# RMSNorm with every row doubled, on one core: two stores split so that the next load can reuse the buffer early

## Chip, cores, metric

One core of a Trainium2 chip. The metric is the device time of one execution in microseconds (us). One program is run several times; "span" is the profiled part of one execution, about 2 us shorter than the time.

## Reference

```python
x: [8, 512, 2048] float32, gamma: [2048] float32
x_rep  = np.repeat(x, 2, axis=1)                       # every row twice
rms    = np.sqrt((x_rep ** 2).mean(axis=-1, keepdims=True) + 1e-6)
output = x_rep / rms * gamma                            # [8, 1024, 2048]
```

So 33.55 MB are read and 67.11 MB written, with little arithmetic between.

## The kernel before

The 4096 rows are cut into eight tiles of 128 partitions times 4 rows. A tile's buffer holds eight rows (64 KB) per partition: x is loaded into rows 4 to 7, the scaled rows are written to rows 0, 2, 4, 6 and copied to 1, 3, 5, 7, and one transfer of 8.39 MB stores all eight. There are three buffers. All transfers are issued from SyncE, in one queue.

```python
K = 4; R = 2
rows = ctx.enter_context(tc.tile_pool(name="rows", bufs=3))

def new_tile():
    ys.append(rows.tile([P, K * R, D], f32, name="y"))

def load(i, k0, k1):
    nc.sync.dma_start(
        out=ys[i][:, K * (R - 1) + k0 : K * (R - 1) + k1, :], in_=x_t[i, :, k0:k1, :]
    )

def store(i):
    nc.sync.dma_start(out=out_t[i], in_=ys[i].rearrange("p j d -> p (j d)"))
# ... total, square, reduce, root, scale, repeat: the arithmetic ...

cuts = [0, *range(D // 4, D + 1, D // 8)]          # seven pieces of gamma
load(0, 0, H)
for c0, c1 in zip(cuts[:-2], cuts[1:-1]):
    gamma_piece(c0, c1)
load(0, H, K)
gamma_piece(cuts[-2], cuts[-1])
# ... gamma is spread over the partitions by TensorE ...
load(1, 0, K)
load(2, 0, K)
# ...
by_rows(0, whole)                                   # each of these ends in store(i)
two = mixed(sums(1, 1), shared, ahead=(2, 1))
mixed(two, shared)
for j in (3, 4, 5):
    new_tile()                                      # the buffers of 0, 1, 2
    load(j, 0, K)
by_rows(3, shared)
_, _, ss = mixed(sums(4, H), whole, ahead=(5, 0))
for j in (6, 7):
    new_tile()                                      # the buffers of 3, 4
    load(j, 0, K)
# ... tile 5 in another way, then tiles 6 and 7 ...
```

## Time and profile before

| | before |
|---|---|
| time, median of the first 3 runs | 239.29 us (239.11 to 239.78) |
| span | 237.1 us |
| busiest engine | VectorE, 132.9 us |
| queue's packets, share of 16 engines' span | 98.6% |

Bytes over the span is 425 GB/s, and the row of transfer engines is full. Whether the transfers leave holes is read from the order of issues and landings, which the prediction shows. Besides the page the trace holds a record of each packet (start, duration, size) and of each increment of a semaphore (a counter on which engines wait) by a transfer; 16 increments, one from each transfer engine, make one landing.

In the lines of profiles below, SP is SyncE, ACT ScalarE and DVE VectorE, and a q behind a name stands for what that engine issues. A line of a timeline gives start and duration in us, engine, line of the kernel, operation, output<-input and count; brackets hold the idle time before, and what ended it. A line of waits gives the total in us, the number of waits and the longest.

### The profile page before, as it was taken

The page shows a single profiled execution, that of the slowest core. Times are in us where ns is not written, and L with a number is a line of the kernel's source. Part 1 is how long each engine was busy: PE and PEld are TensorE (multiplying, and loading weights), DVE is VectorE, ACT ScalarE, POOL GpSimd, SP SyncE. Part 2 cuts the span into 40 slices and gives each one's busy share as a digit, 9 for nine tenths or more (in the row PEclk, how much of TensorE's full clock was granted, in tenths as well). Part 3 has the DMA queues.
Part 4 walks back from the last instruction along what each step waited for, and adds up shares of the span by engine and source line. Part 5 has one row for each costly group of instructions (what it writes and reads, how often), then busy time and mean ns, then how long its engine had stood idle before and what let it go on. Part 6 is the DMA issues. An engine that isn't in the chain of part 4 may idle for free. (4 is left out here: it accounts for less than half of the span.)

```text
span 237.1 us, 246 instructions
## 1 busy us (share of the span) xinstructions
PE 7.2 (3%) x8; PEld 2.3 (1%) x8; DVE 132.9 (56%) x45; ACT 92.6 (39%) x48; POOL 13.0 (5%) x20
## 2 busy tenths in 40 slices
PE   0650000000000000000000000000000000000000
PEld 0210000000000000000000000000000000000000
DVE  0049997997950000039979994094067997980000
ACT  2681957600600000098995003900599760230000
POOL 0000002002000000000020002005302002000000
DMA  7999999899898989999998989899998989899994
GB/s 263 441 448 442 437 448 509 376 398 486 354 531 354 531 354 431 398 415 437 442 531 354 531 354 509 376 387 415 437 531 354 531 354 509 376 486 398 420 464 177
DMA packets 2462, 100.67 MB, mean 425 GB/s; under 512 B 279, under 2 KB 285, under 8 KB 286
## 3 DMA queue, kind: packets, MB, share of 16 engines
q1 hardware_dynamic: 2462, 100.67, 98.6%
HBM read 33.56 MB, written 67.11 MB: 425 GB/s over the span
## 5 line engine op out<-in xcount | busy, mean ns | idle before, releaser
L87 DVE SCALAR_TENSOR_TENSOR y<-y,ss,gamma_b 128x2048 f32<-128x2048 f32 x28 | 64.7, 2345 | 10.4 <-POOL ss L83 7.4
L74 DVE TENSOR_REDUCE ss<-y 128x3 f32<-128x6144 f32 (+2 forms) x6 | 41.4, 6902 | 10.9 <-ACT y L69 10.9
L69 ACT ACTIVATE y<-y 128x6144 f32<-128x6144 f32 (+2 forms) x6 | 33.6, 5604 | 22.9 <-DMA y<-in_x_dram 22.9
L63 ACT ACTIVATE sq<-y 128x2048 f32<-128x2048 f32 x13 | 24.4, 1875 | 42.1 <-DMA y<-in_x_dram 41.9
L94 ACT COPY y<-y 128x4096 f32<-128x4096 f32 (+1 forms) x7 | 23.5, 3358 | 32.1 <-DVE y L87 32.1
L140 DVE RECIPROCAL ss<-ss 128x2 f32<-128x2 f32 x4 | 0.6, 161 | 49.0 <-ACT ss L139 49.0
L94 DVE COPY y<-y 128x4096 f32<-128x4096 f32 (+1 forms) x6 | 18.0, 3004 | 0.2
L192 ACT ACTIVATE y<-y,ss 128x2048 f32<-128x2048 f32 x4 | 7.8, 1993 | 18.8 <-POOL ss L83 18.8
L196 DVE TENSOR_TENSOR y<-y,gamma_b 128x8192 f32<-128x8192 f32 x1 | 8.7, 8687 | 9.3 <-ACT y L192 9.3
L80 POOL TENSOR_SCALAR ss<-ss 128x4 f32<-128x4 f32 x6 | 1.2, 194 | 170.4 <-DVE ss L74 170.4
L127 PE MATMUL gamma_b<-gamma_row,ones 1*128 1x512 f32 x8 | 7.2, 1080 | 8.1 <-DMA gamma_row<-in_gamma_dram 8.1
L94 POOL COPY y<-y 128x6144 f32<-128x6144 f32 x1 | 5.3, 5304 | 16.6 <-DVE y L196 16.6
L83 POOL TENSOR_TENSOR ss<-ss,power_t 128x4 f32<-128x4 f32 x6 | 6.1, 1009 | 0.5
L127 PEld LDWEIGHTS gamma_b<-gamma_row,ones 1*128 1x128 f32 x8 | 2.3, 319 | 11.5 <-issue 10.2
L63 ACT ACTIVATION_READ_ACCUMULATOR sq<-y 128x1 f32 x13 | 2.4, 187 | 0.0
L118 ACT ACT_TABLE_LOAD x1 | 1.3, 1283 | 0.7 <-PEq L221 0.7
L139 ACT ACTIVATE ss<-ss,eps_t 128x2 f32<-128x2 f32 x4 | 1.2, 296 | 0.2
L113 POOL MEMSET ones<- 1x128 f32 x1 | 0.2, 195 | 0.3 <-POOLq L221 0.3
L221 POOL MEMSET const-float32-0.0<- 128x1 f32 x1 | 0.1, 99 | 0.2 <-issue 0.2
L221 POOL MEMSET const-bfloat16-1.0<- 128x1 bf16 x1 | 0.1, 102 | 0.0
L221 POOL MEMSET const-uint8-127<- 128x1 uint8 x1 | 0.1, 102 | 0.0
L221 POOL MEMSET const-float32-1.0<- 128x1 f32 x1 | 0.1, 99 | 0.0
(2 smaller groups left out, 0.2 us busy)
## 6 DMA issues: line engine op xcount, KB each, us to landing
y<-in_x_dram SPq DMA_DIRECT2D x7, 4096.0 KB, 38.7
y<-in_x_dram SPq DMA_DIRECT2D x2, 2048.0 KB, 9.8
out_dram<-y SPq DMA_DIRECT2D x8, 23.2
gamma_row<-in_gamma_dram SPq DMA_DIRECT2D x6, 1.0 KB
gamma_row<-in_gamma_dram SPq DMA_DIRECT2D x1, 2.0 KB
```

The costliest lines, as they stand in the source:

```text
L63: nc.scalar.activation(out=sq[:], in_=ys[i][:, x_at + k, :], func=Act.Square, accum_out=ss[:, k : k + 1])
L69: nc.scalar.activation(out=ys[i][:, k0:k1, :], in_=ys[i][:, x_at + k0 : x_at + k1, :], func=Act.Square)
L74: nc.vector.tensor_reduce(out=ss[:, k0:k1], in_=ys[i][:, k0:k1, :], op=Alu.add, axis=mybir.AxisListType.X)
L80: nc.gpsimd.tensor_scalar(out=at, in0=at, scalar1=inv_d, scalar2=eps, op0=Alu.mult, op1=Alu.add)
L83: nc.gpsimd.tensor_tensor(out=at, in0=at, in1=power_t[:, k0:k1], op=Alu.pow)
L87: nc.vector.scalar_tensor_tensor(out=ys[i][:, R * k, :], in0=ys[i][:, x_at + k, :], scalar=rstd[:, k : k + 1], in1=gamma_b[:], op0=Alu.mul ...
L94: copy(out=y_r[:, k0:k1, 1, :], in_=y_r[:, k0:k1, 0, :])
L118: nc.scalar.preload_act_table(Act.Sqrt)
L127: nc.tensor.matmul(gamma_b[:, c0 : c0 + bank], ones[:], gamma_row[:, c0 : c0 + bank], start=True, stop=True)
L139: nc.scalar.activation(out=at, in_=at, func=Act.Sqrt, scale=inv_d, bias=eps_t[:])
L192: nc.scalar.activation(out=ys[5][:, R * k, :], in_=ys[5][:, x_at + k, :], func=Act.Copy, scale=ss[:, k : k + 1])
L196: nc.vector.tensor_tensor(out=y_r[:, :, 0, :], in0=y_r[:, :, 0, :], in1=gamma_b[:].rearrange("p (k d) -> p k d", k=1).to_broadcast([P, K, ...
```

## The change

Intent: in the old order a load takes the buffer whose store was issued longest ago. In the new one loads 3 and 6 take the buffer stored last, that of tiles 2 and 4. So that they need not wait for all of that store, it is cut into seven rows and one: the load waits for the seven, and the one is to keep the transfer engines busy while the load is issued. Further, buffers are assigned by hand, and gamma comes in five pieces in place of seven.

```diff
-    def store(i):
-        nc.sync.dma_start(out=out_t[i], in_=ys[i].rearrange("p j d -> p (j d)"))
+    def store(i, j0=0, j1=K * R):
+        nc.sync.dma_start(
+            out=out_t[i, :, j0 * D : j1 * D], in_=ys[i][:, j0:j1, :].rearrange("p j d -> p (j d)")
+        )
+
+    def store_open(i):
+        store(i, 1)
+        store(i, 0, 1)
-    cuts = [0, *range(D // 4, D + 1, D // 8)]
+    cuts = [0, D // 4, D // 2, 3 * D // 4, 7 * D // 8, D]
-    mixed(two, shared)
-    for j in (3, 4, 5):
-        new_tile()
+    mixed(two, shared, store=store_open)
+    for j, like in ((3, 2), (4, 0), (5, 1)):
+        ys.append(ys[like])
         load(j, 0, K)
-    _, _, ss = mixed(sums(4, H), whole, ahead=(5, 0))
-    for j in (6, 7):
-        new_tile()
+    _, _, ss = mixed(sums(4, H), whole, ahead=(5, 0), store=store_open)
+    for j, like in ((6, 4), (7, 3)):
+        ys.append(ys[like])
         load(j, 0, K)
```

(`mixed` takes `store` as an argument; that line is left out.)

More of the change, by code (lines that the diff above doesn't have):

```diff
@@ L161, in sums, with mixed @@
         return i, by_row, ss
-    def mixed(given, copies, ahead=None):
+    def mixed(given, copies, ahead=None, store=store):
         i, by_row, ss = given
```

## The prediction

> **What bounds the kernel now.** I read the page's busy shares first, then the DMA rows, then the issue queue of SyncE and what ends its waits, and last the trace's records of single DMA packets and of the semaphore increments that tell of landings. From the page:
>
> ```profile
> span 237.1 us, 246 instructions
> PE 7.2 (3%) x8; PEld 2.3 (1%) x8; DVE 132.9 (56%) x45; ACT 92.6 (39%) x48; POOL 13.0 (5%) x20
> DMA  7999999899898989999998989899998989899994
> q1 hardware_dynamic: 2462, 100.67, 98.6%
> HBM read 33.56 MB, written 67.11 MB: 425 GB/s over the span
> ```
>
> No compute engine is busy over 56%. The DMA row is full from the second slice to the last but one, and its packets fill 98.6% of the 16 engines' span. So either the transfers themselves are the bound, or small holes between them are; a row of tenths cannot tell which. The timeline of SyncE's queue, in four windows (start, duration, what is issued), can:
>
> ```profile
> 68.43 0.33 SPq L56 DMA_DIRECT2D out_dram<-y  x1
> 68.87 0.41 SPq L51 DMA_DIRECT2D y<-in_x_dram  x1
> 71.27 0.34 SPq L51 DMA_DIRECT2D y<-in_x_dram  x1
> 90.76 0.33 SPq L51 DMA_DIRECT2D y<-in_x_dram  x1
> ...
> 116.79 0.34 SPq L56 DMA_DIRECT2D out_dram<-y  x1
> 136.42 0.34 SPq L56 DMA_DIRECT2D out_dram<-y  x1
> 139.10 0.34 SPq L51 DMA_DIRECT2D y<-in_x_dram  x1
> 158.71 0.34 SPq L51 DMA_DIRECT2D y<-in_x_dram  x1
> ```
>
> They are, in order, store 2 and loads 3, 4 and 5; then stores 3 and 4 and loads 6 and 7 (tiles counted from 0). The load at 71.27 follows the landing of store 1 (last increment 71.26), the one at 90.76 store 2 (90.69), 139.10 store 3 (139.09), 158.71 store 4 (158.65). These look like costly waits, and the table of SyncE's waits sums them:
>
> ```profile
> SPq L56 <- DVE y L94: 116.8, 6, 25.6
> SPq L51 <- DMA out_dram<-y: 42.6, 4, 19.2
> ```
>
> But all transfers are in one queue, and each is issued before the queue has run dry. Last increments of each transfer's semaphore, in queue order: load 1 22.80, load 2 32.57, stores 0 to 2 51.95, 71.26, 90.69, loads 3 to 5 100.27, 110.00, 119.71, stores 3 and 4 139.09, 158.65, loads 6 and 7 168.34, 178.05, stores 5 to 7 197.36, 216.66, 235.95. Every load (4.19 MB) takes 9.6 to 9.8 us after its predecessor and every store (8.39 MB) 19.3 to 19.6. Whether it was issued 20 us early (load 3) or 2.7 us early (store 4 at 136.42, behind store 3 that landed at 139.09) makes no difference: no wait shows through. From the second half of load 0 (13.06) to the end there are 7 loads and 8 stores, 23 units of 4.19 MB in 222.89 us: 9.69 us a unit, 433 GB/s. The packet records say the same: a 64 KB packet takes 2418 ns, a 32 KB one 1213, a 16 KB one 611, which is 9 ns plus 36.75 ns per KB of 1000 bytes, and on an engine the next starts when the last ends. So the bound is bytes through the 16 DMA engines. All that is not this is about 3 us before the stream is at speed (the first load issued at 0.72, first packets at 1.73, their first round slowed from 611 ns to 0.85 to 1.6 us) and about 1 us after the last landing.
>
> **What the Trainium skill says.** "DMA: Bandwidth & Descriptors", section Specifications, gives a fabric ceiling of 435 GB/s and an HBM limit per core of about 358. The trace agrees with the first (433) and not with the second as the limit here. The same page, "Anatomy of one DMA", says that DMA engines do not wait on semaphores: the wait is on the issuing sequencer, and a transfer's fixed cost is mostly the write receipt. The trace agrees: at the end of store 3 the engines start the next packet at 138.12 to 138.70 and the increments come at 138.58 to 139.09, about 0.4 us later, and SyncE issues within 0.01 to 0.07 us of the last one. "Latency and other measured facts" on that page gives about 0.6 us to the first byte for a transfer issued from SyncE; here the first load needs 1.01 us to its earliest packet and about 1.6 to the latest engine's first. I use the trace's numbers. "Why a DMA increments its semaphore by 16 and not by 1" says only the full 16 means landed, so a wait ends with the slowest engine; the trace has 16 increments per transfer spread over 0.3 to 0.7 us.
>
> **The change, part by part.**
> Removed: nothing of the x and output traffic; 100.67 MB stay, 24 units of 4.19 MB, 232.6 us at 9.69. No compute instruction changes in kind or number.
>
> Start: gamma comes in five pieces in place of seven, load 1 no longer waits for a free semaphore (issued right after load 0, about 3.3 us in place of 8.4). But the engines have load 0's second half until about 12.1 us, when load 1's first packets start without a hole. The gamma packets fall on one engine: 84 ns for 2 KB and 46 for 1 KB, so 84 + 6 x 46 = 360 ns before and 3 x 84 + 2 x 46 = 344 after, less two completion packets. Gain: 0.0 to 0.1 us.
>
> Stores 2 and 4 are split into seven rows and one. Per engine a 64 KB packet becomes one of 56 KB (9 + 2107 = 2116 ns) and one of 8 KB (310 ns): 8 x 2426 = 19.41 us in place of 8 x 2418 = 19.34. With a further completion packet that is about 0.1 us per split, 0.2 us for two.
>
> Waits: load 3 goes into tile 2's buffer and load 6 into tile 4's. Before, these two were issued behind the store that was still in the queue (68.87 behind 68.43; 139.10 behind 136.42), nearly 20 us ahead of their turn. Now each is issued only when the seven rows have landed. What keeps the engines fed meanwhile is the one row: 8 x 310 ns = 2.48 us on each engine. Let the first engine end the seven rows at X. By the end of store 3 above, all have ended by X + 0.58 and the semaphore is full at X + 0.97; issue follows within 0.07; first packets, by load 0, 1.0 to 1.6 us later: X + 2.0 to X + 2.6. The engines run out of the row at X + 2.48 to X + 3.06. The margin is about 0.5 us, and it shrinks if a transfer that arrives so late begins with slow packets as load 0 did (up to 1 us over, about 0.6 in the middle). I choose 0.15 us of hole per place, 0 to 0.9 possible, so 0.3 for two.
>
> The other loads: 4, 5 and 7 wait for stores 0, 1 and 3, which landed at 51.95, 71.26 and 139.09 or so, long before their issue. They go out within 1 us of loads 3 and 6. Order in the queue and order of tiles stay as they were. Compute: an engine moves on about 0.4 us before its increment, so by the first increments of their predecessors stores 0 to 4 are issued 1.7 to 2.2 us before the first engine runs out and store 5 1.3 us (175.60 against 176.9); that is just enough for the start of 1.0 us, and no hole shows. The work ahead of each starts from the same landings, so this moves with the stream. Row 0 of tile 3 is written only after the one-row store has landed, which is before load 3 has.
>
> Sum: + 0.2 + 0.3 - 0.1 = + 0.4 us on 239.29: 239.7 us.
>
> **The rivals.** First: the 42.6 us of SyncE's waits on stores are partly exposed, and a load that starts 2.4 us earlier, twice, or load 5 issued with load 3, gains up to 4.8 us: 234.5. For it speaks only the table of waits; against it that landings are 9.7 and 19.3 us apart throughout, the load at 90.76 landing 9.71 us after its predecessor. Second: the handover runs dry. If receipt and start cost 1 us more than at the places I measured, each store-to-load turn opens about 1 to 1.5 us: 241.5 to 242.5. For it speaks that I have no case in the trace of a load issued so late; against it the two measured halves, 1.0 and 1.6 us, which cover the worst engine. Third: the freed start gains. If the slow first 3 us came from gamma's small packets or from SyncE's busy queue, up to 1 us could come back: 238.5. Against it: the first gamma packet is at 7.48 us, long after the slow stretch, so it is start-up and stays.
>
> **Range and chances.** Most outcomes lie between a change that costs nothing with the 0.1 us gained (239.0 with the scatter of 239.11 to 239.78) and two holes of 0.5 to 0.8 us (240.9). Faster by 2% means 234.5, and only some 6.7 us of the time (239.29 less 232.6) are not bytes at full rate, most of it start and end; I give 0.01. Slower by 2% means 244.1, two holes of over 2 us; 0.02.
>
> **What would show it.** Right: DMA share and the steps of 9.7 and 19.3 us between landings unchanged, seven rows landing about 17 us after their predecessor, load 3 issued within 0.1 us of that (near 88.3), its landing 12.1 to 12.7 us after the seven rows' landing (2.48 + 9.7 and the hole). Wrong if that step is over 13.5 us, if the landing of load 1 moves by over 0.5 us, or if some load other than 3 and 6 is issued late. A fall below 238 us would refute the bound itself.

## The result, and the profile after

239.97 us (median of 6, 239.52 to 240.86) against 239.65 (median of 6 of the kernel before beside it). The ratio is 1.002, with a 95% interval of 0.9997 to 1.0042: the same, and inside the range foretold (ratios are the mean time of one kernel's runs over that of the other's of the same rounds, so not quite the ratio of the medians). Executions over 1.5% slower than the fastest of the same kernel are left out of the means.

The page after, its lines that answer to those of before:

```profile
span 237.7 us, 245 instructions
PE 7.2 (3%) x8; PEld 2.3 (1%) x8; DVE 132.9 (56%) x45; ACT 92.6 (39%) x48; POOL 13.0 (5%) x20
DMA  7999999899999979999998989999998989999894
q1 hardware_dynamic: 2746, 100.67, 98.5%
HBM read 33.56 MB, written 67.11 MB: 423 GB/s over the span
```

The engines do the same work; there are 284 more packets, and their share of the span is as full. (Single digits of the row differ because a packet counts in the slice in which it starts, so one digit proves nothing.) SyncE's queue after, in several windows of the timeline:

```profile
3.23 5.07 SPq L51 DMA_DIRECT2D y<-in_x_dram  x2
...
68.45 0.84 SPq L56 DMA_DIRECT2D out_dram<-y  x2
88.01 1.31 SPq L51 DMA_DIRECT2D y<-in_x_dram  x3
...
136.75 0.34 SPq L56 DMA_DIRECT2D out_dram<-y  x1
156.29 0.85 SPq L51 DMA_DIRECT2D y<-in_x_dram  x2
```

A line "x3" spans from the first of three issues to the end of the last. The first line holds loads 1 and 2: load 1 now goes out at 3.23 us, load 2 when load 0's first half has landed. Store 2 goes out in two parts from 68.45. Load 3 no longer stands behind it, but waits until 88.01, 0.02 us after the last increment of the seven rows (87.99), and loads 4 and 5 follow at once. The same at 156.29 (0.06 us after 156.23) for loads 6 and 7.

What the late issue costs is seen at the engine that waits for the load. ScalarE's first work on tiles 3 and 6, before:

```profile
100.35 1.88 ACT L63 ACTIVATE sq<-y 128x2048 f32<-128x2048 f32 x1 [35.27 <-DMA y<-in_x_dram]
168.43 5.32 ACT L69 ACTIVATE y<-y 128x6144 f32<-128x6144 f32 x1 [14.25 <-DMA y<-in_x_dram]
```

and after:

```profile
100.69 1.88 ACT L71 ACTIVATE sq<-y 128x2048 f32<-128x2048 f32 x1 [35.58 <-DMA y<-in_x_dram]
168.75 5.32 ACT L77 ACTIVATE y<-y 128x6144 f32<-128x6144 f32 x1 [14.24 <-DMA y<-in_x_dram]
```

Start 0.34 and 0.32 us later. The handover is almost free. The second figure contains the first, and does not grow because a landing goes by the slowest engine: from the first to the last increment of load 6 it was 0.74 us before and 0.55 after. By the mean over the engines the last packets of loads 3 and 6 start 0.22 and 0.65 us later.

The packet records say where the rest is. On each engine the kept-back row's eight packets of 8 KB take 309 ns each, and the first packet of load 3 follows with no gap (row ends at 89.51 to 90.04, first load packets start at 89.51 to 90.05). But the first two load packets are slow: by the mean over the engines the third starts 2.89 us after the first, where two packets take 2.43. A hole need not look like idle time: here it is inside the first packets. Why these are slow is not shown. It looks like a wait for data: at all eight late loads (two each in the change, e8_after_again, e1_no_row and e2_half_row) the second packets start 3.04 to 3.14 us after the issue by the mean over the engines, whether the first ones started 1.1 or 1.7 us after it.

For all the runs below I use one number, the **turn**: by the mean over the 16 engines, how much later the load's last packets start than they would if, from the start of the store's last large packet on, all packets took their usual time and followed without a gap. Each trace has two turns, at load 3 and at load 6. Before they cost 0.23 and 0.07 us, although the load had long been in the queue; after, 0.43 and 0.46.

### The profile page after: what moved, and what is told of

Read it like the earlier page. It is cut to its first block, busy times and chain, and to the rows that moved or that the text cites. A ratio compares the mean times of both kernels' runs of the same rounds, so it can differ in the third digit from the quotient of the medians.

```text
span 237.7 us, 245 instructions
## 1 busy us (share of the span) xinstructions
PE 7.2 (3%) x8; PEld 2.3 (1%) x8; DVE 132.9 (56%) x45; ACT 92.6 (39%) x48; POOL 13.0 (5%) x20
## 2 busy tenths in 40 slices
DMA packets 2748, 100.69 MB, mean 424 GB/s; under 512 B 309, under 2 KB 311, under 8 KB 314
```

## The experiments

Eight kernels, on two chips, in two sets of four. Each set's kernels share the runs of the kernel before: 239.44 us in the first (median of 11), 239.46 in the second (median of 11). The seven of them whose loads stay in the one queue are in the table; e6_two_queues stands below.

| run | what lies behind the store when the load is issued | turns, us | time, us | ratio to before (95%) |
|---|---|---|---|---|
| before | the load itself, queued | 0.23, 0.07 | 239.4 to 239.7 | 1 |
| e5_start_only | the load itself, queued | 0.27, 0.28 | 239.47 | 1.0002 (0.9986 to 1.0019) |
| e7_light | the load itself, queued | 0.21, -0.02 | 239.78 | 1.0015 (1.0 to 1.003) |
| e4_split_only | one row, and the load queued | 0.32, 0.43 | 239.72 | 1.0008 (0.999 to 1.0026) |
| e3_two_rows | two rows, 4.9 us | 0.33, 0.32 | 239.39 | 1.0002 (0.9984 to 1.0019) |
| the change | one row, 2.47 us | 0.43, 0.46 | 239.97 | 1.002 (0.9997 to 1.0042) |
| e8_after_again | one row, 2.47 us | 0.49, 0.52 | 239.63 | 1.0012 (0.9993 to 1.0032) |
| e2_half_row | half a row, 1.27 us | 1.57, 1.37 | 241.46 | 1.0085 (1.0065 to 1.0104) |
| e1_no_row | nothing | 2.67, 2.58 | 244.07 | 1.0195 (1.0173 to 1.0216) |

### No row kept back

```diff
     def store_open(i):
-        store(i, 1)
-        store(i, 0, 1)
+        store(i)
```

> The changed kernel with tiles 2 and 4 stored whole; loads 3 and 6 still go into those buffers, so they wait for the whole store and nothing lies behind it in the queue. Theory (the kept-back row is what feeds the engines during the handover, and the stream of transfers is the bound): each engine stands idle from the end of its last store packet to the late load's first packet. By the traces that is landing 0.97 us after the first engine's end, issue within 0.02, first packets 1.0 to 1.5 us after it, so about 2.0 us of idle time per engine at each of the two places, and some 0.4 us of slow first packets; total 4 to 5 us more than before, 243.5 to 244.5 us, and the landing of load 3 about 12.0 us after store 2's in place of 9.6. Rival (waits of loads are hidden anyway, as 42.6 us of them were before; the changed kernel's 0.2% are the split's extra packets): same as before within 0.3 us.

Measured: 244.07 us, ratio 1.0195, so 4.7 us more, as the theory has it. The timeline of SyncE and ScalarE, of this kernel:

```profile
68.34 0.33 SPq L56 DMA_DIRECT2D out_dram<-y  x1
90.63 1.29 SPq L51 DMA_DIRECT2D y<-in_x_dram  x3
102.86 1.88 ACT L70 ACTIVATE sq<-y 128x2048 f32<-128x2048 f32 x1 [37.87 <-DMA y<-in_x_dram]
```

Store 2 lands at 90.62, load 3 is issued at 90.63, and its data is there at 102.76, 12.14 us after the store, where the kernel before needed 9.58. By the packet records the engines end the store between 89.50 and 90.28 and start load 3 between 91.61 and 92.62: 2.1 us of idle time by the mean, and 0.56 us more in slow first packets. At load 6 it is 1.9 and 0.66. The rival is out: take away the cover and the wait shows in full.

### Half a row

```diff
     def store_open(i):
-        store(i, 1)
-        store(i, 0, 1)
+        store(i, 0.5)
+        store(i, 0, 0.5)
```

(and the slices of `store` are taken in elements)

> The changed kernel with half a row kept back in place of one. Theory: the cover falls from 2.48 us to about 1.27 (8 packets of 4 KB), so about 1.2 us of new hole at each of two places: 2 to 2.6 us more than the changed kernel, 242 to 242.8 us. Rival (one row was far more than the handover needs): same as the changed kernel, 239.9.

Measured: 241.46 us, ratio 1.0085. Load 3 is issued at 89.46 (88.01 in the change), and ScalarE's work on it starts at 101.88 (100.69):

```profile
89.46 1.29 SPq L51 DMA_DIRECT2D y<-in_x_dram  x3
101.88 1.88 ACT L72 ACTIVATE sq<-y 128x2048 f32<-128x2048 f32 x1 [36.84 <-DMA y<-in_x_dram]
```

The direction is right, the size was put too high: 1.5 us over the changed kernel by the medians (1.8 over its repeat), not 2 to 2.6. The turns grew by 1.1 and 0.9 us, not 1.2. I had taken all of the missing cover as loss; by the turns about a sixth of it did not show.

### Two rows

```diff
     def store_open(i):
-        store(i, 1)
-        store(i, 0, 1)
+        store(i, 2)
+        store(i, 0, 2)
```

> The changed kernel with two rows kept back in place of one: cover 4.9 us. Theory: no hole can be left; the third round of load 3's packets starts 2.42 us after the first in place of 2.89. What stays is the cost of the split and a queued turn from store to load (0.08 to 0.25 us in the kernel before). So 0.2 to 0.5 us under the changed kernel and 0.0 to 0.3 over the kernel before. Rival (the 0.2% come from the extra small packets): no faster than the changed kernel, rather slower.

Measured: ratio 1.0002. Load 3 is issued at 85.72 in place of 88.01, 4.3 us ahead of its first packets, and its third round of packets starts 2.44 us after the first, so the slow first packets are gone as the theory says. The gain over the changed kernel, 0.24 to 0.43 us by the ratios, is in the expected range, but the intervals overlap: by the clock alone it is not shown. The turns of 0.33 and 0.32 stay above the kernel before: a second row of cover takes off only the last 0.1 to 0.2 us.

### The split alone, in the old order of buffers

```diff
-    for j, like in ((3, 2), (4, 0), (5, 1)):
+    for j, like in ((3, 0), (4, 1), (5, 2)):
-    for j, like in ((6, 4), (7, 3)):
+    for j, like in ((6, 3), (7, 4)):
```

> The changed kernel (split stores, five gamma pieces, fixed buffers) with the buffers taken in the old order, tiles 3, 4, 5 in those of 0, 1, 2 and tiles 6, 7 in those of 3, 4, so that loads 3 and 6 wait for stores long done and stand in the queue ahead of their turn. Theory: only the split's packets are left, 0.07 us each plus completion packets: 0.0 to 0.3 us over the kernel before, no hole behind store 2 or 4. Rival (the split itself costs the 0.2%): as slow as the changed kernel, with the step from store 2's second part to load 3 still near 10.1 us.

Measured: ratio 1.0008. Load 3 is in the queue long before its turn again. There is no slow start of the load (third round 2.42 us after the first), yet the turns are 0.32 and 0.43, so the split has a cost of its own, more than its packets' 0.06 us: the last three small packets before the load took 333, 411 and 528 ns at the first place and 343, 456 and 541 at the second, by the mean over the engines, in place of 309. In the kernel before the last 64 KB packets of store 2 took 2656 ns in place of 2418, also with the load queued behind. So part of a turn is paid by the store's last packets when the load is already there, and by the load's first ones when it is late. Expected "no hole behind store 2 or 4" was right for idle time and a little short for this. The rival (the split is all of it) named the step from the row to load 3 as its sign, still near 10.1; it is 9.69 between landings (10.11 in the change), but the row itself lands 2.74 us after the seven in place of 2.48. So its sign did not come, though part of the cost now lies ahead of the landing of the row. By the clock the rival is not excluded; by the turns the split makes about 0.2 us each and the late issue about 0.1.

### Gamma in five pieces alone

```diff
-    cuts = [0, *range(D // 4, D + 1, D // 8)]
+    cuts = [0, D // 4, D // 2, 3 * D // 4, 7 * D // 8, D]
```

(in the kernel before)

> The kernel before with gamma in five pieces, nothing else. Theory: load 1 is issued near 3.2 us in place of 8.4, and nothing comes of it, since the engines have load 0 until about 12 us: 0.0 to 0.1 us faster, load 1 lands within 0.1 us of 22.80. Rival (the start holds hidden time): 0.5 us or more faster, load 1 landing before 22.3.

Measured: ratio 1.0002. Load 1 lands at 22.65 in place of 22.80, a shade over the 0.1 us foretold and far from the rival's 22.3. Its two lines of SyncE's timeline and of ScalarE's show how an issue 5 us earlier comes to nothing:

```profile
3.14 5.18 SPq L51 DMA_DIRECT2D y<-in_x_dram  x2
22.67 5.32 ACT L69 ACTIVATE y<-y 128x6144 f32<-128x6144 f32 x1 [5.38 <-DMA y<-in_x_dram]
```

In the kernel before the same work of ScalarE started at 22.82.

### Loads 3 to 5 on a second queue

```diff
-    def load(i, k0, k1):
-        nc.sync.dma_start(
+    def load(i, k0, k1, queue=nc.sync):
+        queue.dma_start(
...
-        load(j, 0, K)
+        load(j, 0, K, nc.scalar)
```

(in the kernel before, for tiles 3, 4, 5)

> The kernel before with loads 3, 4 and 5 issued from ScalarE's queue in place of SyncE's, so that loads and stores run side by side on the engines. Theory (each engine moves 27.1 GB/s whatever the direction): the bytes take as long as before; load 3 lands earlier and store 2 later; same within 0.5 us if no store comes too late. Rival (reads and writes have rates of their own, and the one queue keeps them from overlapping): the stretch with both moves more than 460 GB/s and the whole is 3 to 10 us faster.

Measured: 245.09 us, ratio 1.0242 (1.0224 to 1.0259). Neither time came true; the theory's "if no store comes too late" was not met. The rate is what the run was for, and it is plain in the packet records: from 80 to 104 us both queues have packets on the engines, and together they move 433 to 434 GB/s, with 16 packets under way at almost any time. That is the rate of one queue alone. In the first stretch with both, from 66 to 77 us, it is less, 391 GB/s: 32 KB packets take up to 2755 ns there in place of 1213, and about 1.1 us per engine is lost. Why is not shown. So reading beside writing gained nothing here; that no other mix or order would beat the bound is not shown by one run. Most of the loss has another cause, seen in the timelines of ScalarE and SyncE:

```profile
106.37 0.34 ACTq L51 DMA_DIRECT2D y<-in_x_dram  x1
106.75 1.88 ACT L63 ACTIVATE sq<-y 128x2048 f32<-128x2048 f32 x1 [41.91 <-DMA out_dram<-y]
...
123.19 0.33 SPq L56 DMA_DIRECT2D out_dram<-y  x1
```

In ScalarE's program load 5 stands before the arithmetic of tile 3. Load 5 waits for store 2, which shared the engines and landed at 106.27 in place of 90.69; the arithmetic of tile 3, loaded by 95.88, started 11 us after that, at 106.75. So store 3 was issued at 123.19 in place of 116.79, and its first packets started at 124.08, after most engines had had nothing since about 119.4: 4.2 us without packets by the mean over the engines.

### Less compute (wrong results on purpose)

```diff
     def repeat(i, k0, k1, copy=nc.scalar.copy):
+        if i > 2:
+            return
```

(with whole stores, the old order of buffers and gamma in five pieces)

> Wrong results on purpose: in tiles 3 to 7 the second rows are not copied (old contents are stored), with whole stores and the old order of buffers. It takes 2.3 to 8 us of VectorE, ScalarE or GpSimd work out ahead of each of stores 3 to 7. Theory (bytes are the bound, compute is 1.3 to 2.2 us ahead of need or more): same as before within 0.3 us. Rival (the compute chain ahead of some store is the bound): 2 us or more faster.

Measured: 239.78 us, ratio 1.0015 (1.0 to 1.003): not faster. VectorE's busy time falls to 123.8 us and ScalarE's to 76.6, and stores 3 and 4 are issued 2.2 and 6.8 us earlier than before:

```profile
PE 7.3 (3%) x8; PEld 2.3 (1%) x8; DVE 123.8 (52%) x42; ACT 76.6 (32%) x43; POOL 7.7 (3%) x19
114.56 0.34 SPq L56 DMA_DIRECT2D out_dram<-y  x1
129.65 0.34 SPq L56 DMA_DIRECT2D out_dram<-y  x1
```

They wait in the queue instead. No compute chain ahead of stores 3 to 7 holds the time; tiles 0 to 2 were left as they were.

### The changed kernel again

> The changed kernel again, for a second trace and a closer time. Theory: 0.2 to 0.7 us over the kernel before; at load 3 and load 6 the third round of packets again starts 2.8 to 2.9 us after the first, in place of 2.42; stores 6 and 7, which took 0.2 and 0.4 us longer than before in the first trace, take 19.3 us each, if that was scatter of the run. Rival: stores 6 and 7 are long again, so that part of the cost is of the change.

Measured: ratio 1.0012, and the third rounds start 2.94 and 2.98 us after the first, a little over the 2.8 to 2.9 expected. Stores 6 and 7 land 19.39 and 19.41 us after their predecessors, against 19.49 and 19.66 in the first trace of the change and 19.30 and 19.29 before. So most of that was scatter of one run; a tenth stays that I can't place.

## Why the prediction was right

**The bound.** Bytes through the 16 transfer engines, 433 GB/s, was right, and two runs tested it from outside: with less compute nothing was won, and with reads beside writes the rate reached 433 to 434 and no more.

**Start.** Foretold 0.0 to 0.1 us gained from gamma and load 1; the run of that part alone has a ratio of 1.0002, and load 1 landed 0.15 us earlier in its trace. No gain that the clock can tell.

**Split.** Foretold 0.1 us each. The packets came out at the worked values (2116 and 309 ns). With the slowed last packets it is nearer 0.2 each: queued turns with whole stores are 0.17 by the mean of six (before, e5_start_only, e7_light), with a split 0.35 by the mean of four (e4_split_only, e3_two_rows), and 0.06 for the packets' own time comes on top. The turns scatter by up to 0.3 us, so the size is rough. This term was set low, at half, because I had not seen that a turn from store to load costs anything in a full queue.

**Hole.** Foretold 0.15 us each, 0 to 0.9 possible. Late but covered turns are 0.475 by the mean of four (the change twice), 0.125 more than with the load queued. The three steps were right: issue 0.02 and 0.06 us after the last increment (within 0.07 was foretold); idle time without cover 2.1 and 1.9 us where 2.0 was worked out; cover 2.47 us. That the slow first packets would show was also foretold, with about 0.6 us in the middle; without cover they were 0.56 and 0.66. The step between landings named as the test, 12.1 to 12.7 us from the seven rows to load 3, came out at 12.59, and at load 6 at 12.43.

**Sum.** Foretold +0.4 us; the ratios of the two measurements make it +0.5 and +0.3, the turns of the traces 2 x (0.475 - 0.17 + 0.06) = 0.7. Both intervals hold zero, from about 0.1 and 0.2 us under it to 1.0 and 0.8 over, and all three figures. So the change is the same by the clock, and that it costs some tenths rests on the traces. That 0.4 met the clock's figures so well is in part luck: by the traces the split, worth 0.2 in the sum, is nearer 0.5.

**Rivals.** The first (waits of 42.6 us are partly exposed) is out: it asked for up to 4.8 us, and no time was won. The waits themselves are about as long; the table after has two in place of four:

```profile
SPq L51 <- DMA out_dram<-y: 37.3, 2, 18.7
```

The second (the handover runs dry) is what e1_no_row and e2_half_row show when the row is taken away; with it the row just suffices. The third (gain at the start) is out by e5_start_only.

No version here beats both kernels. The kernel before has whole stores and loads queued ahead of their turn, which is the cheapest turn measured.

## What to carry to other kernels

In the kernel before, whose one queue was never empty, 42.6 us of waits on the issuing engine cost nothing that the landings show; so look whether each transfer is issued before its predecessor has drained, not how long the issuer waited. If a load must reuse the buffer just being stored, let something stand behind the store: measure the handover (here 2.6 us with nothing behind it) and keep back at least that much transfer time. Where a buffer freed earlier is at hand, as here, let the load take that and queue it ahead. And read a hole in the durations of the first packets as well as in idle time.

## What the Trainium skill lacked or had wrong

- "DMA: Bandwidth & Descriptors", section Bandwidth: "For HBM↔SBUF transfers the HBM side (~358) binds". One core alone held 433 GB/s in loads and in stores, and from 80 to 104 us of e6_two_queues in both at once, near the fabric ceiling of 435 that the page gives. The same section measures 425 on a core whose neighbour is idle, and so does the page "HBM Reference" (about 425 for a core that streams alone): both agree better, so the sentence lacks the condition.
- The first of these pages, "Latency and other measured facts": about 0.6 us to the first byte, without a word on where the count begins. From the start of the issuing instruction the earliest packet comes after 1.01 us here (load 0) and 0.98 and 0.97 (e1_no_row). From its end, 0.38 and 0.34 us later, it is 0.63, 0.64 and 0.63, which agrees. The mean over the engines is 0.3 and 0.2 us more in e1_no_row.
- No page that I found gives, for transfers issued from SyncE, the cost of handing a buffer from a store to a load: 2.67 and 2.58 us of stream time in e1_no_row, of which 0.56 and 0.66 are slow first packets.
- No page that I found says that a turn from store to load costs something in a full queue: 0.17 us by the mean of six turns.
- No page that I found gives a packet's time by size as found here: 309, 611, 1213, 2116 and 2418 ns for 8, 16, 32, 56 and 64 KB.
